# Completing each late unit of a mixture of experts in itself, with whole tiles at the end and stores from two queues

## The chip, the cores and the metric

The kernel runs on one core of a Trainium2 chip. The metric is the device time of one execution in microseconds (us). Five engines run their own instruction streams in order and wait for each other through semaphores: TensorE (PE in the rows, PEld for its weight loads), VectorE (DVE), ScalarE (ACT), GpSimd (POOL) and SyncE (SP). DMAs are issued by SP, ACT and POOL and are carried out by 16 DMA engines that the core has to itself.

## The reference

One layer of a streaming encoder on x of 512 tokens by 1024 (float32). Everything before the experts (modulated norm, convolution group, latent attention, output projection, residual) is the same in both kernels but for the queue that loads x first. The part that matters here is the mixture of experts:

```python
def hier_moe(h, w_group, b_group, w_expert, b_expert, w_gate_e, w_up_e, w_down_e):
    ...                                   # top-1 group of 4, top-2 experts of its 8: gates [512, 32]
    y = jnp.zeros_like(h)
    for e in range(N_EXPERTS):            # 32 experts, D_MODEL 1024, D_EXPERT 256
        a = jax.nn.silu(h @ w_gate_e[e]) * (h @ w_up_e[e])
        y = y + gates[:, e:e + 1] * (a @ w_down_e[e])
    return y
# out = x + g_f * hier_moe(norm(x) * (1 + sc_f) + sh_f)
```

Each expert has 1 MB of gate, 1 MB of up and 1 MB of down weights; all 32 are loaded, some 100 MB. Each token goes to two experts.

## The kernel before, in words

The front of the kernel (to about 290 us) computes the modulation, the projections, attention, convolution and the routing. Then the experts come in 12 **units**, in the order `eeellsllsxss`: e and l units hold two experts with 64 places for tokens each, s units four experts with 32 places, and the x unit two experts with 64 + 32 and 32 places. A unit's tokens are gathered from DRAM into a tile of 128 rows (indirect DMA, POOL), and then go through these steps (the class `Unit`, and `combine`):

- `Unit(...)`, L1443: eight transposes on TensorE turn the 128 x 1024 rows; ACT (L1446) and VectorE (`complete`, L1457 and L1458) scale and shift them.
- `gate_up`, L1469: for each of eight slices of the 1024 inputs one matmul per piece of the unit, gate and up side by side in 512 columns. The first four slices need the expert's weight tile "part 0", the last four "part 1". Then silu on ACT (L1472) and a product on VectorE (L1474).
- `turn`, L1481: two transposes of the product, and a copy on ACT (L1483).
- `down`, L1495, in two halves of 512 output columns: matmuls, then VectorE scales with the gate (L1498), ACT rounds to float32r (L1499) and the remainder is taken (L1500, on POOL, in the last unit on VectorE), so that a high and a low part stand in a tile.
- `combine`, L1512: with a one-hot matrix of the unit's tokens (`one_hot`, VectorE, L1451) TensorE spreads the rows to the 512 tokens, in 8 tiles (2 column halves by 4 token tiles), and VectorE adds each tile to x (L1515). Two PSUM banks `f` are used by turns; the last unit uses four (two of them named `tr`). In the last unit each tile is stored by a DMA as soon as it is added (L1517).

The loop at L1560 writes these steps in the order in which each engine runs them: gate and up of unit n, the transposes of unit n + 1, down of unit n - 1, the turn of unit n, and then four tiles of a `combine`, which adds units in pairs. For the last unit the loop runs the rest of the combine before it, places the combine of the unit before between the halves of gate and up, and then runs down half, combine half, down half, combine half.

Weights come through SP alone (`loads_upto`, `load_keys`, L997), in the order part 0, part 1, down of each unit, into a ring of 4 and slots of 15 tiles of 1 MB (`room`); a load waits until its tile was read, and for the eighth load before it. A gate/up tile takes two DMAs of 512 KB, a down tile one of 1 MB. Those of the last unit are cut in halves and interleaved between experts (`LAST`, `cuts`).

Of the kernel before, what the change touches and what calls it, by code (L numbers as in the profile page):

```python
# [41 lines left out]
def hybrid_block(ctx: ExitStack, tc: tile.TileContext, A, out, dbg=None, stop=None):  # L42
    nc = tc.nc
    pe, act, dve, pool, sp = nc.tensor, nc.scalar, nc.vector, nc.gpsimd, nc.sync
# [88 lines left out]

    def load_x():
        ts = []
        for i in range(2):
            xt = S([128, 2, 1024])
            for s in range(2):
                sp.dma_start(xt[:, s, :], xv[:, 2 * i + s, :])
            ts.append(xt)  # L140
        return ts

    X = load_x()

# [822 lines left out]

    def load(key, n):

        e, part = key  # L970
        o = Wtile()
        o.room = room.pop(0)
        shape = [128, 2, 1024] if part == "d" else [128, 2, 4, 256]
        o.t = (W if o.room == "r" else S)(shape)
        if isinstance(e, int):
            pick = lambda w: w[e]
        else:
            if part == 0:
                reg_of[e] = sp.value_load(od[0:1, e[1]:e[1] + 1], min_val=0, max_val=31)
            pick = lambda w: w[bass.ds(reg_of[e], 1)].rearrange("e p a b -> (e p) a b")  # L980
        if part == "d":
            ds = [(o.t[:, :, cs], pick(wd)[:, :, cs]) for cs in cuts(1024, n)]
        else:
            ds = [(o.t[:, k, js], pick(w)[:, 4 * part + js.start:4 * part + js.stop, :])
                  for js in cuts(4, n) for k, w in ((0, wg), (1, wu))]
        Wt[key] = o
        per = len(ds) // n
        return [ds[i:i + per] for i in range(0, len(ds), per)]

    def cuts(m, n):  # L990
        return [slice(i, i + m // n) for i in range(0, m, m // n)]

    def load_keys(ks):

        for ds in zip(*[load(key, min(len(ks), 2)) for key in ks]):
            for o, i in sum(ds, []):
                sp.dma_start(o, i)  # L997

# [18 lines left out]
    nxt = [0]  # L1017
    LAST = {(units[-1][2][0], "d"): 4}
    LAST.update({(units[-1][2][i], part): 2 for i in (0, 2) for part in (0, 1)})

    def loads_upto(n):
        while room and nxt[0] < min(n, len(keys)):
            m = LAST.get(keys[nxt[0]], 1)
            if len(room) < m:
                break
            load_keys(keys[nxt[0]:nxt[0] + m])
            nxt[0] += m

# [19 lines left out]
    loads_upto(3)  # L1048
    X[:] = load_x()

# [379 lines left out]
    class Unit:  # L1430
# [3 lines left out]
        def __init__(self, kind, tokf, gate, buf, weights, first=False):  # L1434
            self.pieces, self.gate, self.buf, self.weights = PIECES[kind], gate, buf, weights
            n = self.n = sum(self.pieces[-1][:2])
            self.hg = hg

            chunks = buf.rearrange("p (q j) -> p j q", j=8) if first else buf.rearrange("p (j q) -> p j q", j=8)
            for hf in range(2):  # L1440
                pt = tr()
                for j in range(4):
                    pe.transpose(pt[:, j * n:(j + 1) * n], chunks[:n, 4 * hf + j, :], ident[:n, :n])  # L1443
                if hf == 0:
                    for j in range(4):
                        act.activation(self.hg[:, j, :n], pt[:, j * n:(j + 1) * n], AF.Identity, scale=G2[:, j:j + 1], bias=H2[:, j:j + 1])  # L1446
            self.pt, self.tokf = pt, tokf

# [53 lines left out]

    def combine(us, banks=None, store=False):

        for u_ in us:
            u_.one_hot()
        for hf in range(2):
            for tt in range(4):
                o = banks[tt]() if banks else fb()
                for m, u_ in enumerate(us):  # L1510
# [5 lines left out]
                if store:  # L1516
                    sp.dma_start(out[0, tt * 128:(tt + 1) * 128, 512 * hf:512 * hf + 512], xr)  # L1517
                yield
# [38 lines left out]


    comb, done, side, prev = iter(()), [], over_table(), None
    for n_ in range(len(units)):  # L1560
        last = n_ == len(units) - 1
        if last:
            run(comb)
            run(prev.down())
            comb = combine([prev])
        cur.gate_up(lambda: last and run(comb))
        if n_ == 1:
            run(gate)
        nxt_u = start(n_ + 1)
        if nxt_u:  # L1570
            nxt_u.complete()
        if last:
            cur.turn()
            down, comb = cur.down(dve), combine([cur], (fb, fb, tr, tr), True)
            for hf in range(2):
                run(down, 1)
                run(comb, 4)
            break
        if prev:
            run(prev.down())  # L1580
            done.append(prev)
        cur.turn()
        if len(done) == 2:
            comb, done = combine(done), []
        run(comb, 4)
        if n_ > 1:
            run(side, 1)
        r_ = [Wt[e, part].room for part in (0, 1) for e in units[n_][2]]
        if n_ < 3:
            r_.remove("s")  # L1590
        if n_:
            r_ += [Wt[e, "d"].room for e in units[n_ - 1][2]]
        room += r_
        loads_upto(len(keys))
        prev, cur = cur, nxt_u
    pool_order.close()
# [123 lines left out]
```

## Time and profile before

| | |
|---|---|
| median of 3 runs | 539.66 us (539.51, 542.92, 539.66) |
| profiled execution | 538.74 us, of it 537.1 us from first to last instruction (span) |
| TensorE busy | 488.8 us (91%) |
| VectorE, ScalarE, GpSimd busy | 274.5, 177.7, 124.5 us |
| HBM read | 150.97 MB, 290 GB/s over the span |
| chain of waits that ended last | PE 58%, DMA 19%, DVE 10%, SP's queue 4%, ACT 4% |

A busy share is an average over parts with different limits, and matmuls that wait in the pipeline count as busy. So the stretches and the chain of waits tell more than the 91%. Times in the rows are us from the start of the span.

### The profile page before, as it was taken

The numbers are of one execution on the slowest core, as the hardware profiler recorded it, in microseconds if no ns is written. First come the engines' busy times: TensorE is split into PE (matmuls) and PEld (weight loads), VectorE is DVE, ScalarE is ACT, GpSimd is POOL, SyncE is SP. The second block draws the span as 40 slices with busy tenths as digits, with TensorE's granted clock in tenths as the row PEclk, the third lists the DMA queues.
The fourth block names the chain that finished last, engine by engine and source line by source line (L and its number), as shares of the span: only waits on it lengthen the run. The fifth ranks groups of instructions, "written<-read, shape, count | busy, mean of one in ns | idle before, by whom it ended". The sixth has DMA issues, their size and how long they took to land.

```text
span 537.1 us, 8202 instructions
## 1 busy us (share of the span) xinstructions
PE 488.8 (91%) x2891; PEld 276.2 (51%) x2891; DVE 274.5 (51%) x631; ACT 177.7 (33%) x389; POOL 124.5 (23%) x118
## 2 busy tenths in 40 slices
PE   4989999899999898999998999999999799989962
PEld 4768976535644475788874344444444241424321
DVE  2447789948937765642555234334453150415532
ACT  4233744015675556721545222210222020211010
POOL 3220570008644534100001022211222020101100
PEclk9999999999999889999998999999999899999988
DMA  8999539986951252286878989999999999999973
GB/s 257 302 320 308 169 131 316 378 304 191 264 187 40 69 207 91 80 306 231 324 242 307 324 316 392 333 416 405 384 414 392 418 409 414 411 408 317 338 264 123
DMA packets 61763, 154.42 MB, mean 287 GB/s; under 512 B 7657, under 2 KB 27257, under 8 KB 56080
## 3 DMA queue, kind: packets, MB, share of 16 engines
q1 hardware_dynamic: 58288, 147.03, 77.3%
q0 software_dynamic: 1888, 4.00, 2.3%
q10 hardware_dynamic: 1536, 2.77, 1.4%
q8 instruction: 25, 0.41, 0.3%
q14 instruction: 26, 0.21, 0.1%
HBM read 150.97 MB, written 4.77 MB: 290 GB/s over the span
## 4 chain that ended last, share of the span: by engine, by line
PE 58%; DMA 19%; DVE 10%; SPq 4%; ACT 4%; issue 2%; POOL 1%; DVEq 0%; ACTq 0%; POOLq 0%
PE acc L1469 12%; PE acc L1495 7%; PE f L1512 6%; DMA s<-in_w_up_e_dram 6%; DMA s<-in_w_down_e_dram 5%; PE acc L116 5%; PE acc L118 4%; PE acc L117 4%; DMA s<-in_w_ada_dram 2%; DVE dw L346 2%; PE f L334 2%; SPq L167 2%; DMA w<-in_w_up_e_dram 2%; DMA w<-in_w_ada_dram 2%; PE tr L1443 2%
## 5 line engine op out<-in xcount | busy, mean ns | idle before, releaser
L1469 PE MATMUL acc<-s,gw 128*32 128x512 f32 (+1 forms) x392 | 94.1, 604 | 1.5 <-DMA s<-in_w_up_e_dram 1.5
L116 PE MATMUL acc<-s,s 128*128 128x512 f32 (+3 forms) x160 | 63.3, 395 | 1.0 <-DVE s L774 1.0
L1512 PE MATMUL f<-s,t 128*128 128x512 f32 x184 | 49.5, 417 | 10.7 <-DVE t L1451 8.1
L118 PE MATMUL acc<-s,s 128*128 128x512 f32 (+3 forms) x160 | 58.8, 368 | 0.0
L117 PE MATMUL acc<-s,s 128*128 128x512 f32 (+3 forms) x160 | 58.8, 368 | 0.0
L1469 PE MATMUL acc<-w,gw 128*32 128x512 f32 (+1 forms) x136 | 54.4, 636 | 3.1 <-DMA w<-in_w_up_e_dram 3.0
L1474 DVE TENSOR_TENSOR t<-t,acc 128x256 f32<-128x256 f32 x12 | 5.1, 421 | 92.5 <-ACT t L1472 92.5
L346 DVE SCALAR_TENSOR_TENSOR dw<-s,cwh,dw 128x512 f32<-128x512 f32 x60 | 50.0, 849 | 1.2
L1469 PEld LDWEIGHTS acc<-s,gw 128*32 128x32 f32 (+1 forms) x392 | 24.9, 124 | 49.6 <-issue 49.5
L1472 ACT ACTIVATE t<-acc 128x256 f32<-128x256 f32 x12 | 4.6, 384 | 129.2 <-PE acc L1469 129.2
L1500 POOL TENSOR_TENSOR s<-t,s 128x512 fp32r<-128x512 f32 x22 | 28.5, 1294 | 75.9 <-ACT s L1499 75.5
L1515 DVE TENSOR_TENSOR s<-s,f 128x512 f32<-128x512 f32 x52 | 35.3, 688 | 20.7 <-PE f L1512 20.7
L1512 PEld LDWEIGHTS f<-s,t 128*128 128x128 f32 x184 | 31.7, 191 | 27.0 <-DVE s L1515 7.1
L1495 PE MATMUL acc<-s,t 128*32 128x512 f32 (+1 forms) x200 | 44.7, 599 | 0.5 <-ACT t L1483 0.5
L116 PEld LDWEIGHTS acc<-s,s 128*128 128x128 f32 x160 | 30.2, 189 | 14.8 <-issue 7.9
L1427 POOL DMA_INDIRECT s<-xg,sidx x11 | 11.2, 1022 | 107.0 <-PE tr L1443 76.6
L1499 ACT CAST s<-t 128x512 fp32r<-128x512 f32 x24 | 14.8, 618 | 53.3 <-DVE t L1498 53.3
L118 PEld LDWEIGHTS acc<-s,s 128*128 128x128 f32 x160 | 30.1, 188 | 4.1
L117 PEld LDWEIGHTS acc<-s,s 128*128 128x128 f32 x160 | 30.3, 189 | 3.3 <-issue 0.2
L1498 DVE SCALAR_TENSOR_TENSOR t<-acc,rt,gw 128x512 f32<-128x512 f32 x24 | 18.0, 751 | 24.8 <-PE acc L1495 24.8
L871 ACT ACTIVATE t<-acc,sm,qs 128x128 f32<-128x128 f32 (+3 forms) x32 | 19.7, 617 | 21.9 <-DVE sm L869 18.6
L868 DVE TENSOR_REDUCE sm<-acc 128x1 f32<-128x128 f32 (+3 forms) x32 | 15.5, 486 | 20.1 <-PE acc L867 20.0
(311 smaller groups left out, 814.4 us busy)
## 6 DMA issues: line engine op xcount, KB each, us to landing
s<-in_w_down_e_dram SPq DMA_DIRECT2D x21, 1024.0 KB, 11.3
s<-in_w_gate_e_dram SPq DMA_DIRECT2D x41, 512.0 KB
s<-in_w_up_e_dram SPq DMA_DIRECT2D x41, 512.0 KB, 10.2
w<-in_w_ada_dram SPq DMA_DIRECT2D x16, 1024.0 KB, 9.2
w<-in_w_gate_e_dram SPq DMA_DIRECT2D x15, 512.0 KB
w<-in_w_up_e_dram SPq DMA_DIRECT2D x15, 512.0 KB, 9.3
w<-in_w_down_e_dram SPq DMA_DIRECT2D x7, 1024.0 KB, 4.9
s<-in_w_ada_dram SPq DMA_DIRECT2D x6, 1024.0 KB, 11.4
```

The costliest lines, as they stand in the source:

```text
L116: pe.matmul(o, lh, rh, start=start, stop=False)
L117: pe.matmul(o, lh, rl, start=False, stop=False)
L118: pe.matmul(o, ll, rh, start=False, stop=stop)
L346: dve.scalar_tensor_tensor(dw[:, t, :], u[:, t // 2, k:k + 512], w, dw[:, t, :], op0=OP.mult, op1=OP.add)
L868: dve.tensor_reduce(H["mx"][:, qt:qt + 1], p[:, :n], axis=AX.X, op=OP.max)
L871: act.activation(e[:, :n], p[:, :n], AF.Exp, scale=qs[:, qt, h:h + 1], bias=H["nb"][:, qt:qt + 1], accum_out=H["rs"][:, qt:qt + 1])
L1469: pe.matmul(gu[sl, :], self.hg[:, j, sl], w.t[:, :, j % 4, :], start=(j == 0), stop=(j == 7), tile_position=(0, o_), skip_group_check=True)
L1495: pe.matmul(o[o_:o_ + w_, :], self.aT[:, n * c + o_:n * c + o_ + w_], w.t[:, c, hs], start=(c == 0), stop=(c == 1), tile_position=(0, o_), ...
L1498: dve.scalar_tensor_tensor(yf[:n], o[:n], self.gate, gf[:n, hs], op0=OP.mult, op1=OP.mult)
L1500: eng.tensor_tensor(self.yhl[:n, 1, hs], yf[:n], self.yhl[:n, 0, hs].bitcast(F32), op=OP.subtract)
L1512: pe.matmul(o, u_.ot[:u_.n, tt * 128:(tt + 1) * 128], u_.yhl[:u_.n, k, 512 * hf:512 * hf + 512], start=(m == 0 and k == 0), stop=(m == len ...
L1515: dve.tensor_tensor(xr, xr, o, op=OP.add)
```

## The change

Four things change. (1) From the sixth unit on (`SOON = 5`), down follows the turn of the same unit, and the unit is combined alone: four of its tiles between the halves of the next unit's gate and up, four after the next unit's turn. Units 1 to 4 are still combined in pairs, unit 5 alone. (2) The last unit's weights are loaded as all others, in whole tiles; its one-hot matrix is made ahead of down, and both halves of down are run before the combine. (3) The eight stores go out from SP and ACT by turns. (4) The four first loads of x are issued by ACT instead of SP.

```diff
-    def load_x():
+    def load_x(eng):
...
-                sp.dma_start(xt[:, s, :], xv[:, 2 * i + s, :])
+                eng.dma_start(xt[:, s, :], xv[:, 2 * i + s, :])
...
-    X = load_x()
+    X = load_x(act)
...
         if part == "d":
-            ds = [(o.t[:, :, cs], pick(wd)[:, :, cs]) for cs in cuts(1024, n)]
-        else:
-            ds = [(o.t[:, k, js], pick(w)[:, 4 * part + js.start:4 * part + js.stop, :])
-                  for js in cuts(4, n) for k, w in ((0, wg), (1, wu))]
...
+            return [(o.t, pick(wd))]
+        return [(o.t[:, k], pick(w)[:, 4 * part:4 * part + 4, :]) for k, w in ((0, wg), (1, wu))]
...
-    LAST = {(units[-1][2][0], "d"): 4}
-    LAST.update({(units[-1][2][i], part): 2 for i in (0, 2) for part in (0, 1)})
-
     def loads_upto(n):
         while room and nxt[0] < min(n, len(keys)):
...
+            for o, i in load(keys[nxt[0]]):
+                sp.dma_start(o, i)
+            nxt[0] += 1
...
-    X[:] = load_x()
+    X[:] = load_x(sp)
...
-    def combine(us, banks=None, store=False):
+    def combine(us, banks=(fb,) * 4, store=False):
 
         for u_ in us:
-            u_.one_hot()
+            if not u_.ot:
+                u_.one_hot()
...
-                    sp.dma_start(out[0, tt * 128:(tt + 1) * 128, 512 * hf:512 * hf + 512], xr)
+                    (act if tt % 2 else sp).dma_start(out[0, tt * 128:(tt + 1) * 128, 512 * hf:512 * hf + 512], xr)
...
+    SOON = 5
     comb, done, side, prev = iter(()), [], over_table(), None
     for n_ in range(len(units)):
         last = n_ == len(units) - 1
-        if last:
-            run(comb)
-            run(prev.down())
-            comb = combine([prev])
-        cur.gate_up(lambda: last and run(comb))
+        cur.gate_up(lambda: n_ >= SOON and run(comb, 4))
...
-        if last:
-            cur.turn()
-            down, comb = cur.down(dve), combine([cur], (fb, fb, tr, tr), True)
-            for hf in range(2):
-                run(down, 1)
-                run(comb, 4)
-            break
         if prev:
             run(prev.down())
             done.append(prev)
         cur.turn()
-        if len(done) == 2:
-            comb, done = combine(done), []
-        run(comb, 4)
+        if n_ < SOON:
+            if len(done) == 2:
+                comb, done = combine(done), []
+            run(comb, 4)
+        else:
+            run(comb)
+            if done:
+                run(combine(done))
+            if last:
+                comb = combine([cur], (fb, fb, tr, tr), True)
+                cur.one_hot()
+                run(cur.down(dve))
+                run(comb)
+                break
+            run(cur.down())
+            comb, done = combine([cur]), []
...
-        if n_:
+        if prev:
             r_ += [Wt[e, "d"].room for e in units[n_ - 1][2]]
+        if n_ >= SOON:
+            r_ += [Wt[e, "d"].room for e in units[n_][2]]
         room += r_
         loads_upto(len(keys))
-        prev, cur = cur, nxt_u
+        prev, cur = cur if n_ < SOON else None, nxt_u
```

Line numbers of the changed kernel differ: L1469, L1481, L1495, L1512 and L997 of before are L1451, L1463, L1477, L1495 and L1008 there.

TensorE at the end of unit 11's gate and up (`acc_4181` before), before the change: the eight transposes of unit 12's rows (`tr_...<-ident,s`) are followed by unit 10's down.

```order
L1469 MATMUL acc_4181<-w_4142,gw 32x512
L1443 MATMUL tr_4217<-ident,s_2166 128x128 x4
L1443 MATMUL tr_4226<-ident,s_2166 128x128 x4
L1495 MATMUL acc_4234<-s_3981,t_4113 64x512
L1495 MATMUL acc_4234<-s_3981,t_4113 32x512
L1495 MATMUL acc_4234<-s_3983,t_4113 32x512
```

And the same place with the change (the turn is L1463, combine L1495, down L1477).

```order
L1425 MATMUL tr_4344<-ident,s_2166 128x128 x4
L1425 MATMUL tr_4353<-ident,s_2166 128x128 x4
L1463 MATMUL tr_4360<-ident,t_4341 128x128 x2
L1495 MATMUL f_4365<-s_4215,t_4307 128x512 x2
L1495 MATMUL f_4369<-s_4215,t_4307 128x512 x2
L1495 MATMUL f_4373<-s_4215,t_4307 128x512 x2
L1495 MATMUL f_4377<-s_4215,t_4307 128x512 x2
L1477 MATMUL acc_4382<-w_4128,t_4363 32x512
L1477 MATMUL acc_4382<-s_4130,t_4363 32x512
```

Unit 11's own turn comes right after the transposes, then four tiles of unit 10 alone, and then unit 11's own down; another unit's down no longer stands between.

TensorE at the end of the last unit, before the change: four tiles of the first half (`f`, `tr`) are added between the two halves of down (L1495).

```order
L1495 MATMUL acc_4476<-s_4340,t_4473 32x512
L1512 MATMUL f_4491<-s_4475,t_4489 128x512 x2
L1512 MATMUL f_4496<-s_4475,t_4489 128x512 x2
L1512 MATMUL tr_4501<-s_4475,t_4489 128x512 x2
L1512 MATMUL tr_4506<-s_4475,t_4489 128x512 x2
L1495 MATMUL acc_4511<-s_4337,t_4473 32x512
L1495 MATMUL acc_4511<-w_4338,t_4473 32x512
```

With the change (down is L1477, combine L1495).

```order
L1477 MATMUL acc_4506<-w_4426,t_4485 32x512
L1477 MATMUL acc_4519<-s_4420,t_4485 32x512
L1477 MATMUL acc_4519<-s_4422,t_4485 32x512
L1477 MATMUL acc_4519<-s_4424,t_4485 32x512
L1477 MATMUL acc_4519<-w_4426,t_4485 32x512
...
L1495 MATMUL f_4532<-s_4505,t_4503 128x512 x2
L1495 MATMUL f_4537<-s_4505,t_4503 128x512 x2
L1495 MATMUL tr_4542<-s_4505,t_4503 128x512 x2
L1495 MATMUL tr_4547<-s_4505,t_4503 128x512 x2
L1495 MATMUL f_4552<-s_4505,t_4503 128x512 x2
```

The second half of down (`acc_4519`) now follows the first without a tile of the combine between them, and the eight tiles come after both.

## Rows read from the trace of the kernel before

**Rows 1.** The page's second section: load on the DMA engines in 40 slices.

```profile
DMA  8999539986951252286878989999999999999973
GB/s 257 302 320 308 169 131 316 378 304 191 264 187 40 69 207 91 80 306 231 324 242 307 324 316 392 333 416 405 384 414 392 418 409 414 411 408 317 338 264 123
```

**Rows 2.** Table by stretches: length, each engine's busy time, clock, DMA share, GB/s.

```profile
391.00:484.00 93.00, 86.09 (x436) 31.09 (x434) 29.02 (x46) 15.76 (x38) 13.46 (x11) 0.98 1.02 409
484.00:510.00 26.00, 24.26 (x136) 10.79 (x136) 14.25 (x22) 2.46 (x5) 5.12 (x4) 1.00 0.95 327
```

**Rows 3.** The chain of waits: start, duration, what. From 441 to 474 us.

```profile
441.39 12.37 DMA s<-in_w_down_e_dram
...
464.00 10.15 DMA w<-in_w_up_e_dram
```

**Rows 4.** The list of DMA issues: size of each, median us to landing.

```profile
s<-in_w_up_e_dram SPq DMA_DIRECT2D x41, 512.0 KB, 10.2
...
s<-in_w_up_e_dram SPq DMA_DIRECT2D x12, 256.0 KB, 6.1
```

**Rows 5.** The chain of waits from unit 6 on; the 450.68 row from the timeline.

```profile
368.57 7.00 PE acc L1469 x64
375.57 1.02 PE tr L1443 x8
376.60 3.58 PE acc L1495 x16
...
380.55 3.84 PE f L1512 x16
...
450.68 8.01 PE L1469 MATMUL acc<-s,gw 128*64 128x512 f32 x24
...
478.90 7.99 PE acc L1495 x24
...
503.20 0.68 PE f L1512 x2
...
507.73 1.34 PE f L1512 x4
```

**Rows 6.** The last unit: chain of waits, one stretch (clock 0.50), timeline of DVE.

```profile
514.59 1.97 PE acc L1495 x16
...
516.58 0.76 DVE t L1498
...
518.01 0.69 DVE s L1500
...
519.25 2.04 PE f L1512 x4
...
520.00:522.00 2.00, 2.00 (x7) 1.51 (x6) 1.35 (x2) 0.00 (x0) 0.00 (x0) 0.50 0.00 0
...
528.75 1.28 DVE L1515 TENSOR_TENSOR s<-s,tr 128x512 f32<-128x512 f32 x2
```

**Rows 7.** The stores' line: durations, first and last start; time to landing.

```profile
L1517 SPq DMA_DIRECT2D out_dram<-s x8: 332/350/1158, 521.2 to 530.6; - x8
...
DMA to landing us min/median/max: 2.0/2.7/3.3
```

**Rows 8.** The start: stretches, then the timeline of SP, ACT and PE.

```profile
0.00:5.00 5.00, 1.23 (x4) 0.93 (x4) 0.48 (x4) 1.49 (x2) 1.69 (x7) 1.00 0.61 177
5.00:10.00 5.00, 1.61 (x8) 1.61 (x9) 1.13 (x4) 2.52 (x5) 1.63 (x4) 1.00 0.94 303
...
1.36 1.84 SPq L139 DMA_DIRECT2D s<-in_x_dram  x4
3.24 3.33 SPq L157 DMA_DIRECT2D s<-in_w_ada_dram  x2
...
5.55 1.06 ACT L209 ACTIVATE xh<-s 128x1024 f32<-128x1024 f32 x1 [2.12 <-DMA s<-in_x_dram]
...
27.45 1.92 PE L222 MATMUL tr<-s,cs 128*32 128x256 f32 x28 [1.56 <-DMA s<-in_w_ada_dram]
```

More of the change, by code (lines that the diff above doesn't have):

```diff
@@ L966, in hybrid_block, with load @@
         pass
-    def load(key, n):
+    def load(key):
         e, part = key
@@ L980, in load @@
             pick = lambda w: w[bass.ds(reg_of[e], 1)].rearrange("e p a b -> (e p) a b")
+        Wt[key] = o
         if part == "d":
-            ds = [(o.t[:, :, cs], pick(wd)[:, :, cs]) for cs in cuts(1024, n)]
-        else:
-            ds = [(o.t[:, k, js], pick(w)[:, 4 * part + js.start:4 * part + js.stop, :])
-                  for js in cuts(4, n) for k, w in ((0, wg), (1, wu))]
[L986 to L997, printed above, removed]
+            return [(o.t, pick(wd))]
+        return [(o.t[:, k], pick(w)[:, 4 * part:4 * part + 4, :]) for k, w in ((0, wg), (1, wu))]
     PIECES = {2: [(0, 64, 0), (64, 64, 1)], 4: [(32 * i, 32, i) for i in range(4)],
@@ L1017, in hybrid_block @@
     nxt = [0]
-    LAST = {(units[-1][2][0], "d"): 4}
-    LAST.update({(units[-1][2][i], part): 2 for i in (0, 2) for part in (0, 1)})
     def loads_upto(n):
         while room and nxt[0] < min(n, len(keys)):
-            m = LAST.get(keys[nxt[0]], 1)
-            if len(room) < m:
-                break
-            load_keys(keys[nxt[0]:nxt[0] + m])
-            nxt[0] += m
+            for o, i in load(keys[nxt[0]]):
+                sp.dma_start(o, i)
+            nxt[0] += 1
     dve.scalar_tensor_tensor(G2, G2, 1.0, col("nf"), op0=OP.add, op1=OP.mult)
@@ L1446, in __init__ @@
                         act.activation(self.hg[:, j, :n], pt[:, j * n:(j + 1) * n], AF.Identity, scale=G2[:, j:j + 1], bias=H2[:, j:j + 1])
-            self.pt, self.tokf = pt, tokf
+            self.pt, self.tokf, self.ot = pt, tokf, None
         def one_hot(self):
@@ L1501, in down @@
                 yield
-    def combine(us, banks=None, store=False):
+    def combine(us, banks=(fb,) * 4, store=False):
         for u_ in us:
-            u_.one_hot()
+            if not u_.ot:
+                u_.one_hot()
         for hf in range(2):
             for tt in range(4):
-                o = banks[tt]() if banks else fb()
+                o = banks[tt]()
                 for m, u_ in enumerate(us):
@@ L1571, in hybrid_block @@
             nxt_u.complete()
-        if last:
-            cur.turn()
-            down, comb = cur.down(dve), combine([cur], (fb, fb, tr, tr), True)
-            for hf in range(2):
-                run(down, 1)
-                run(comb, 4)
-            break
         if prev:
```

## The prediction

> **What bounds the kernel now.** I read the page first. Its second section gives the load on the DMA engines in 40 slices of 13.4 us [rows 1]: from the 27th slice on they are full, at 384 to 418 GB/s, until the last four slices sink to 317, 338, 264 and 123. The reader is to see both: a long full stretch, and an end that is not full though nothing but loading is left to do. The table by stretches says it in numbers [rows 2]: from 391 to 484 us the share is 1.02 at 409 GB/s; from 484 to 510 us it is 0.95 at only 327 GB/s.
>
> Then the chain of waits. From 441 to 474 us it consists of loads alone [rows 3]: the last down weights of unit 10 of 12 (units counted from 1; e and l units have 2 experts, s units 4) land at 441.39 + 12.37 = 453.76 us, the last gate and up weights of unit 11 at 464.00 + 10.15 = 474.15 us. Between these lie 16 loads of 512 KB, 8.39 MB in 20.39 us, 411 GB/s. So in the middle TensorE waits for weights and the stream sets the pace. After 474 us the chain is TensorE and what follows it, to the end [rows 5, 6].
>
> Why is the stream slow at the end? The list of DMAs [rows 4] shows the up loads of 512 KB landing a median 10.2 us after issue, those of 256 KB after 6.1 us. The second kind is the last unit's, which are cut in halves. SP keeps eight loads in flight (each waits for the eighth before it): 8 x 0.524 MB in 10.2 us is 411 GB/s, 8 x 0.262 MB in 6.1 us is 344 GB/s. With half the bytes in flight and packets of half the size, the same eight loads don't fill the engines.
>
> **The change part by part.**
>
> *Last unit in whole tiles.* The order of the loads is the same, so up to 474 us I take the stream as it is. Unit 11's down weights (4.19 MB) and the whole of unit 12 (12.58 MB) follow at the measured 411 GB/s: 474.15 + 10.2 = 484.35, and 484.35 + 30.6 = **514.9 us** for the very last tile. Before, at 327 GB/s, the last piece comes at up to 484.35 + 38.5 = 522.8. But the last unit's first half of down began at 514.59 us [rows 6], because in halves the first half needs only half of the tiles. So the load side of this start moves by +0.3 us and no more: what the faster stream gains is used up by waiting for whole tiles. The bounds are 514.9 and, if whole tiles go no faster than halves, 522.8; I take the first, since its rate is that of 16 loads of the same size just before.
>
> The Trainium skill, page "Perfetto Trace Analysis", section "DMA Optimizations", advises splitting a DMA so that some of it starts sooner, where the engines are idle; this change does the opposite. By that rule the last down would start at up to 522.8 and the kernel would gain nothing. The share of 0.95 to 1.02 [rows 2] says the engines are not idle, so the rule's condition isn't met here.
>
> *Units 6 to 12 completed in themselves.* TensorE does the same matmuls, but down follows its own gate and up, and each unit is added to x by itself. Does TensorE still arrive by 514.9? From 368.57 us, where unit 6 starts in both orders [rows 5]:
> - gate and up: six units at 7.00 = 42.0, unit 10 (pieces of 64 and 32) two halves of 8.01 = 16.0;
> - transposes 6 x 1.02 = 6.1; turns 7 x 0.45, with 0.2 each for what they wait, 4.5;
> - down: six times 3.6 = 21.6 (unit 5's among them), unit 10's 8.0;
> - adding units: four tiles of the pair 3 and 4 at 4.1 (3.84 without its wait); unit 5 alone, behind its own down, 1.3 of waiting and 5.9; units 6 to 11, 12 halves of 2.9. A unit alone costs more than half a pair: from 503.20 to 509.07 us it took 5.87 for eight tiles, paced by VectorE's adds, where half a pair's eight took about 3.9.
> The sum is 144, and the last turn has nothing to hide behind (about 1 us): 368.6 + 145 = **513.6 us**. A tie with the stream; I take 514.9, and the range has to hold TensorE some us late. VectorE's 24 additional adds (15 us at 0.64) lie in these halves.
>
> Does this order starve the stream? A load also waits until its buffer was read. Down weights now come free a unit earlier, and by the sum above TensorE finishes the first half of unit 11's gate and up near 484 us and the second near 491, while unit 12's loads into those buffers land from about 497 us (gate and up, after 484.35 and 10.2 for the first half) and 509 us (down) on, and are issued some 10 and 12 us before that, at 487 and 497. So nothing is late, with 3 to 6 us to spare.
>
> *The tail.* Before: down half, scale, round, subtract, one-hot, add four tiles, and only then the second half's down [rows 6], from 514.59 to the last add at 530.03. Now both halves of down run together: 3.6 us. VectorE's scale starts at +1.99, the subtract ends at +4.1 (518.70 - 514.59); the second scale, round and subtract, 2.1 us, end at +6.25; then eight adds at 0.645 (1.28 a pair), bound by VectorE, end at +11.4. Before it was 15.4: **-4.0 us**. Bounds: -4.1, and 0 if TensorE falls to 1.2 GHz, as it did from 519 to 522 us after 2.7 us of waiting [rows 6]: then down takes 7.2 and the eight tiles 8 more.
>
> *Stores from two queues.* From the last add to the end were 7.1 us; the last store was issued 0.6 us after it, and the stores took 2.0 to 3.3 us to land [rows 7]. Now SP and ACT issue by turns, so the last leaves at once: **-1.1 us**, between +1.5 (eight stores in 5 us instead of two groups of four) and -2.
>
> *First loads of x on ACT.* SP's first w_ada load moves from 3.24 to about 1.36 us [rows 8]. ACT's first work on x was at 5.55 us and had waited 2.12 us for it, so the four issues (1.84 us on SP) find room there. The engines' share was 0.61 in the first 5 us, of which 1.4 pass before x is issued at all, and 0.94 in the next 5, so they were nearly full once started. What waits behind is TensorE, 1.56 us at 27.45 us, for w_ada. I take **-0.5 us**, between +0.5 (x arrives later, mixed with w_ada) and -1.9 (all of the earlier issue).
>
> The Trainium skill, page "DMA: Bandwidth & Descriptors", section "Issuing engines are not separate DMA queues", says that DMAs from several engines share the same 16 engines and save only issue time. By it this term would be 0 and the forecast 0.5 us later; the traces of before cannot decide it.
>
> *The rest* (SP's shorter loader, the one-hot set early) costs nothing: it lies under SP's and VectorE's waits.
>
> **Sum.** -0.5 + 0.3 - 4.0 - 1.1 = -5.3 us. The profiled execution took 538.74 (span 537.1), so 533.4 on its own scale; it lies 0.92 under the median of 539.66, so for a median **534.3 us**, 1.0% faster. A measurement here tells about 1% from no change, that is 534.3 and 545.1: the forecast stands on the line.
>
> **Rivals.**
> 1. *The start and the stores give their full amounts* (-1.9, -2): 532.0. For: the chain begins with SP's issues. Against: the share of 0.94. Chance 0.15.
> 2. *The tail doesn't pay*: whole tiles go slower than 411 GB/s, or TensorE waits for the last tile and drops to 1.2 GHz. 2 to 8 us are lost: 536 to 542. For: the engine did drop at 519; against: 16 loads at 411. Chance 0.18.
> 3. *TensorE becomes the bound and the kernel is slower.* From unit 6 on there is no other unit's down between gate/up and turn, and 56 tiles are added one by one on two banks. If VectorE paces a tile at 1.0 instead of 0.73 us (it also has 1.5 us of scaling per unit, and the next unit's activations), 15 us come on top of 513.6: last down at 528.6, time 548. It decides from 514.9 on, and costs over 1% once it is 11 us late. For: 0.73 already is above TensorE's 0.5. Against: that work stands in VectorE's 11 us of gate, turn and down. Chance 0.10.
> The forecast keeps 0.57: from 532 (its terms at their gaining ends) to 538 (TensorE 2 us late at the last down, the stores at +1.5 in place of -1.1). The range for 8 in 10 is 531 to 540: rival 1 less the 0.9 us by which the executions shown scatter (538.74 to 539.66), and up to rival 2 at 5.7 of its 8 us. Faster by over 1%: half of the forecast and rival 1, about 0.44; slower: 0.11; within: 0.45.
>
> **What will show it.** The last unit's up loads should land after about 10 us in place of 6.1, and the rate from 484 to 514 us be about 409. TensorE should hardly wait for weights between 391 and 474. The last down should start at 514 to 516 and the last add come 11 to 12 us later. If that start is past 518 because TensorE arrives late, the sum of matmuls was wrong; if a weight load ends the wait, the rate was.

## The result and the profile after

The changed kernel took **534.95 us** (median of 4 runs, 532.28 to 537.63) beside 540.49 us (4 runs, 539.51 to 542.92) of the kernel before: ratio 0.987 (95% interval 0.983 to 0.991). In a second comparison, with 8 and 31 runs, it was 536.23 beside 541.98, ratio 0.990 (0.987 to 0.994). So it is about 1% faster. The profiled execution took 534.46 us, span 532.9; before it was 538.74 and 537.1. The forecast was 534.3.

The lines of the program have moved: gate and up are now L1451, turn L1463, down L1477, scaling L1480 to L1482, the matmuls that add a unit to x L1495, the adds L1498, the stores L1500.

The page's second section [rows 1]:

```profile
GB/s 270 302 320 310 156 122 325 368 330 174 247 228 9 73 237 92 75 271 220 361 197 321 292 355 371 317 405 413 398 415 408 411 413 411 410 417 409 414 162 164
```

The full stretch now reaches to the 38th slice at 398 to 417 GB/s, and then the load stops at once: the sinking slices of before (317, 338, 264) are gone. The stretches say the same [rows 2] (columns: length, busy time of TensorE, its weight loads, VectorE, ScalarE, GpSimd, clock, DMA share, GB/s):

```profile
391.00:484.00 93.00, 87.36 (x433) 30.01 (x434) 39.37 (x63) 15.22 (x34) 15.06 (x13) 1.00 1.02 412
484.00:510.00 26.00, 24.09 (x174) 8.80 (x164) 11.65 (x18) 3.53 (x9) 3.27 (x3) 1.00 1.02 409
516.00:533.00 17.00, 6.59 (x33) 3.00 (x25) 7.58 (x12) 1.24 (x2) 0.00 (x0) 0.80 0.35 129
```

409 GB/s stand where 327 stood. The packets of the DMAs differ too, from 484 to 510 us, first before, then with the change:

```profile
DMA packets 4613, 8.50 MB, mean 327 GB/s; under 512 B 481, under 2 KB 481, under 8 KB 4609
DMA packets 2426, 10.65 MB, mean 409 GB/s; under 512 B 268, under 2 KB 268, under 8 KB 1987
```

Before, the packets that carry weights have 2 KB in this stretch and take 0.094 us in the mean; now most have 4 KB and take 0.163 us. In the list of DMAs all up loads are of 512 KB now [rows 4]:

```profile
s<-in_w_up_e_dram SPq DMA_DIRECT2D x49, 512.0 KB, 10.9
```

The chain of waits around the last unit [rows 6]:

```profile
512.54 1.34 PE f L1495 x4
513.88 2.24 PE acc L1477 x16
...
516.14 0.76 DVE t L1480
...
520.30 3.60 DVE s L1498 x6
...
524.36 0.73 DVE s L1498 x2
```

The last down begins at 513.88 (514.59 before), directly behind TensorE's own matmuls. The loads of [rows 3] have left the chain, which now shares the span so (page, fourth section; DMA was 19%):

```profile
PE 69%; DVE 13%; DMA 6%; ACT 4%; SPq 3%; issue 2%; POOL 1%; DVEq 0%; ACTq 0%; POOLq 0%
```

The last add ends at 525.09, 11.2 us later; before it was 15.4. And TensorE's list of waits, from 376 us to the end (us in total, times, longest):

```profile
PE f L1495 <- DVE s L1498: 5.4, 16, 0.8
PE tr L1463 <- DVE gw L1439: 3.9, 5, 0.8
```

Two more waits of 1 us follow; none for weights is among them (only the weight loads of the last down sat idle 0.2 us for a DMA). New is the second line: five turns wait 0.78 us each for VectorE, which completes the next unit's rows. The stores [rows 7] and the start [rows 8]:

```profile
L1500 SPq DMA_DIRECT2D out_dram<-s x4: 332/338/349, 520.9 to 524.5; - x4
L1500 ACTq DMA_DIRECT2D out_dram<-s x4: 338/342/348, 521.5 to 525.1; - x4
...
DMA to landing us min/median/max: 2.1/3.3/4.5
```

```profile
1.35 1.95 SPq L157 DMA_DIRECT2D s<-in_w_ada_dram  x2
...
0.91 2.43 ACTq L139 DMA_DIRECT2D s<-in_x_dram  x4
6.74 1.06 ACT L209 ACTIVATE xh<-s 128x1024 f32<-128x1024 f32 x1 [0.19 <-DMA s<-in_x_dram]
```

The last store leaves with the last add (525.1). From the last add to the end are 7.8 us, not 6.0 as forecast (7.1 before). The view gives a time to landing for some of the stores only; by the semaphore events in the trace the last store lands 4.6 us after the last add and the end of the span comes 3.2 after that. Before these were 5.1 and 2.0.

What SP does behind its last store is in the rows of its own instructions, before and with the change:

```profile
L1632 SPq COMPARE_BRANCH  x1: 53/53/53, 532.0 to 532.0; - x1
L1632 SPq EVENT_SEMAPHORE  x9: 17/17/17, 534.8 to 535.4; - x9
L1716 SPq EVENT_SEMAPHORE  x14: 17/28/28, 535.5 to 537.1; - x14
```

```profile
L1620 SPq COMPARE_BRANCH  x1: 53/53/53, 526.0 to 526.0; - x1
L1620 SPq EVENT_SEMAPHORE  x9: 17/17/17, 529.1 to 529.7; - x9
L1704 SPq EVENT_SEMAPHORE  x14: 17/28/28, 529.8 to 532.8; - x14
```

It reads a count and jumps (`COMPARE_BRANCH`) over the code for tokens that found no place in a unit, stands still, and then goes through the last waits. In the trace the jump ends 0.98 us after the last add (before 2.04), SP stands for 3.03 us behind it (2.78) and a second time for 1.38 us among the last waits (before not at all), and the remaining waits take 2.4 (2.3): 7.8 us and 7.1. The wait for the last store is passed at 529.71, at the moment of its landing (529.69; before 535.17 and 535.15) and in step with the waits around it.

At the start, the first w_ada load goes out at 1.35 instead of 3.24 us, yet x arrives 1.2 us later than before (6.74, not 5.55) and unit 6 starts at 368.53 (368.57 before).

### The profile page after: what moved, and what is told of

Read it like the earlier page. It is cut to its first block, busy times and chain, and to the rows that moved or that the text cites. A ratio compares the mean times of both kernels' runs of the same rounds, so it can differ in the third digit from the quotient of the medians.

```text
span 532.9 us, 8170 instructions
## 1 busy us (share of the span) xinstructions
PE 486.2 (91%) x2891; PEld 272.9 (51%) x2891; DVE 289.0 (54%) x655; ACT 178.3 (33%) x389; POOL 124.4 (23%) x118
## 4 chain that ended last, share of the span: by engine, by line
PE 69%; DVE 13%; DMA 6%; ACT 4%; SPq 3%; issue 2%; POOL 1%; DVEq 0%; ACTq 0%; POOLq 0%
PE acc L1451 18%; PE acc L1477 9%; PE f L1495 8%; PE acc L116 5%; PE acc L118 4%; PE acc L117 4%; DVE s L1498 3%; DVE dw L346 2%; PE f L334 2%; DMA s<-in_w_ada_dram 2%; PE tr L1425 2%; DMA w<-in_w_ada_dram 2%; PE f L574 2%; PE acc L899 2%; DMA xg<-t 2%
## 5 line engine op out<-in xcount | busy, mean ns | idle before, releaser
L1451 PE MATMUL acc<-s,gw 128*32 128x512 f32 (+1 forms) x408 | 92.5, 597 | 0.0
L1498 DVE TENSOR_TENSOR s<-s,f 128x512 f32<-128x512 f32 x76 | 49.6, 685 | 35.9 <-PE f L1495 35.9
L1495 PE MATMUL f<-s,t 128*128 128x512 f32 x184 | 54.4, 425 | 8.8 <-DVE s L1498 5.4
L1451 PEld LDWEIGHTS acc<-s,gw 128*32 128x32 f32 (+1 forms) x408 | 24.6, 122 | 46.7 <-issue 44.8
L1451 PE MATMUL acc<-w,gw 128*32 128x512 f32 (+1 forms) x120 | 48.2, 622 | 0.0
L1482 POOL TENSOR_TENSOR s<-t,s 128x512 fp32r<-128x512 f32 x22 | 28.2, 1281 | 85.1 <-ACT s L1481 79.1
L1495 PEld LDWEIGHTS f<-s,t 128*128 128x128 f32 x184 | 30.0, 188 | 33.0 <-DVE s L1498 16.9
L1477 PE MATMUL acc<-s,t 128*64 128x512 f32 (+1 forms) x184 | 44.5, 598 | 0.0
L1481 ACT CAST s<-t 128x512 fp32r<-128x512 f32 x24 | 14.8, 618 | 63.7 <-DVE t L1480 56.7
L1480 DVE SCALAR_TENSOR_TENSOR t<-acc,rt,gw 128x512 f32<-128x512 f32 x24 | 18.0, 750 | 25.0 <-PE acc L1477 25.0
## 6 DMA issues: line engine op xcount, KB each, us to landing
s<-in_w_ada_dram SPq DMA_DIRECT2D x6, 1024.0 KB, 11.2
```

The lines of the kernel that those rows point to most:

```text
L1451: pe.matmul(gu[sl, :], self.hg[:, j, sl], w.t[:, :, j % 4, :], start=(j == 0), stop=(j == 7), tile_position=(0, o_), skip_group_check=True)
L1477: pe.matmul(o[o_:o_ + w_, :], self.aT[:, n * c + o_:n * c + o_ + w_], w.t[:, c, hs], start=(c == 0), stop=(c == 1), tile_position=(0, o_), ...
L1480: dve.scalar_tensor_tensor(yf[:n], o[:n], self.gate, gf[:n, hs], op0=OP.mult, op1=OP.mult)
L1482: eng.tensor_tensor(self.yhl[:n, 1, hs], yf[:n], self.yhl[:n, 0, hs].bitcast(F32), op=OP.subtract)
L1495: pe.matmul(o, u_.ot[:u_.n, tt * 128:(tt + 1) * 128], u_.yhl[:u_.n, k, 512 * hf:512 * hf + 512], start=(m == 0 and k == 0), stop=(m == len ...
L1498: dve.tensor_tensor(xr, xr, o, op=OP.add)
```

## The experiments

**Theory A**, mine after the result: the gain is the tail of the last unit, which needs whole tiles; TensorE and the stream of weights tie at the last down; start and stores gave nothing. Its rivals are named in the expectations. The marks are in this table; each is of one execution, and so are differences between them. From the profiled execution: "last add" counts from the start of unit 6 to the end of the last add, "landing" from there until the last store has landed (semaphore events), "rest" from there to the end of the span.

| kernel | median, us | ratio to before (95%) | unit 6 starts | last add | landing | rest |
|---|---|---|---|---|---|---|
| before | 541.98 / 540.84 / 542.50 | 1 | 368.57 | 161.5 | 5.1 | 2.0 |
| the change | 534.95 | 0.987 (0.983 to 0.991) | 368.53 | 156.6 | 4.6 | 3.2 |
| e0, the change again | 536.23 | 0.990 (0.987 to 0.994) | 369.34 | 157.1 | 4.5 | 3.3 |
| e1, x on SP | 537.61 | 0.993 (0.990 to 0.997) | 367.45 | 156.9 | 4.5 | 3.5 |
| e2, stores from SP | 537.01 | 0.992 (0.989 to 0.995) | 369.20 | 157.4 | 4.6 | 4.2 |
| e4, before + whole tiles | 544.49 | 1.006 (1.003 to 1.010) | 370.52 | 162.1 | 5.2 | 5.1 |
| e3, change in halves | 537.51 | 0.991 (0.988 to 0.994) | 368.05 | 159.7 | 4.6 | 2.0 |
| e5, before + whole + tail | 538.95 | 0.996 (0.993 to 0.999) | 370.45 | 157.3 | 4.6 | 4.8 |
| e6, early turn | 537.25 | 0.991 (0.987 to 0.994) | 370.29 | 157.5 | 4.6 | 3.2 |
| e7, early turn, down in halves | 536.73 | 0.992 (0.988 to 0.995) | 368.87 | 156.4 | 4.1 | 5.0 |
| e9, turn in another bank | 537.25 | 0.989 (0.984 to 0.994) | 369.24 | 159.3 | 4.5 | 3.9 |
| e10, the same, down in halves | 535.30 | 0.987 (0.983 to 0.991) | 369.60 | 154.2 | 4.6 | 4.7 |
| e12, half of the stores (2 runs) | 533.39 | 0.984 (0.978 to 0.990) | 368.82 | 157.3 | 4.4 | 2.4 |

e0, e1, e2 and e4 ran beside the first median of before, e3 to e7 (without e4) beside the second, e9 to e12 beside the third.

**e0_change_again.** No edit.

> The changed kernel once more, as the measure for the runs beside it. Theory A (the 5.8 us gained are the last unit's tail, 15.4 to 11.2 us, and 0.7 of an earlier last down; start and stores gave nothing): ratio to the kernel before 0.987 to 0.991, unit 6 begins at 368.3 to 368.8 us, last down at 513.5 to 514.5, last add 11.0 to 11.5 later, 7 to 8 us from there to the end. Theory B (the gain is for the most part luck of the profiled execution, a scatter of 532 to 538 in the runs so far): ratio 0.993 or more.

Ratio and end (7.8 us) are as A says. Unit 6 began at 369.34, 0.5 later than it allows, the last down at 514.66 (145.3 after unit 6), 0.2 later, and the last add came 11.8 after that, 0.3 more. B's 0.993 lies just inside this interval (to 0.994) and outside the first one (to 0.991): that the gain is luck of one execution is unlikely. How far the first 368 us differ from execution to execution was new.

**e1_x_on_sp.** The start undone.

```diff
-    X = load_x(act)
+    X = load_x(sp)
```

> The changed kernel with the first loads of x back on SP, nothing else undone. Theory A (the start gives nothing, because what the weights of ada gain is used up before unit 6): the same as the changed kernel within 0.5 us, unit 6 at 368.3 to 368.9. Theory C (the earlier issue is worth its 0.5 to 1.9 us, and something else has cost the same in the changed kernel): unit 6 at 369.0 to 370.5, and 0.5 to 1.9 us longer.

Neither, as it was put: unit 6 came *earlier*, at 367.45. The chain of waits and the stretches of e1 tell why:

```profile
48.15 1.86 PE tr L222 x32
...
367.45 3.57 PE acc L1451 x32
...
66.00:290.00 224.00, 210.28 (x1302) 137.73 (x1301) 148.55 (x371) 105.43 (x222) 66.28 (x64) 1.00 0.64 218
290.00:366.00 76.00, 72.22 (x405) 33.25 (x405) 29.66 (x78) 21.91 (x56) 17.72 (x16) 1.00 0.95 352
```

and the same of e0:

```profile
47.34 1.86 PE tr L222 x32
...
369.34 3.57 PE acc L1451 x32
...
66.00:290.00 224.00, 211.35 (x1293) 138.74 (x1292) 147.47 (x360) 105.53 (x222) 65.64 (x64) 0.98 0.64 215
290.00:366.00 76.00, 72.69 (x403) 33.31 (x403) 29.17 (x81) 21.91 (x56) 16.93 (x16) 0.98 0.94 345
```

At the transposes of w_ada's last part (L222) e1 is 0.8 us late. Then e1's clock stays at 1.00, in e0 it is 0.98 in both stretches, and e1 needs 319.30 us from there to unit 6 instead of 322.00. The clock of one execution hides the start. So I compared that row in all traces: with x on ACT (nine) 47.34 to 48.00, mean 47.58; with x on SP (before, e1, e4, e5) 47.40, 48.15, 48.30 and 49.56, mean 48.35. The start may be worth **0.8 us** there, with four scattered values on one side; before's profiled execution was the earliest of its kind. At unit 6 nothing of it shows: the means are 369.10 (nine) and 369.25 (four), within a scatter of 3 us. The medians (537.61 against 536.23, intervals of the ratios overlapping) differ C's way. So neither A's "nothing" nor C's amount is shown.

The Trainium skill ("DMA: Bandwidth & Descriptors", "Issuing engines are not separate DMA queues") says that a second issuing engine saves only issue time. Here the earlier issue was 1.9 us of SP's time, of which 0.8 may be seen at 47 us; that the term is then 0, as I had worked out, does not follow from the page.

**e2_stores_sp.** The stores undone.

```diff
-                    (act if tt % 2 else sp).dma_start(out[...], xr)
+                    sp.dma_start(out[...], xr)
```

> The changed kernel with all eight stores of the last unit issued by SP. Theory A (the end is set by how long the last stores take to land, 4.5 us, and not by their issue): last add to end 7.5 to 8.5 us, against 7.8 with two queues, time the same within 0.7 us. Theory D (two queues save the wait in the queue, as forecast, 1.1 us): last add to end 8.9 or more, time 1.1 us longer. If it is under 7.3, two queues cost something.

Last add to end is 8.7 us, between A's bound (8.5) and D's (8.9), 1.0 longer than with two queues; the median is 0.8 longer (intervals overlapping). The last store lands 4.6 us after the last add, as with two queues: the second queue saves nothing that lands. But the end does not wait for the landing, which was A's reason:

```profile
L1620 SPq COMPARE_BRANCH  x1: 53/53/53, 528.3 to 528.3; - x1
L1620 SPq EVENT_SEMAPHORE  x9: 17/17/17, 531.1 to 533.7; - x9
```

SP passes the wait for the last store at 533.67, 2.5 us after it landed (531.20); in e4, e5, e7 and e10 it is 2.8 to 3.4. What counts is when SP is done with the jump: here 1.69 us after the last add and in e5, also from SP alone, 2.01; in the eight kernels with eight stores from two queues 0.96 to 1.11. So at that mark the second queue saves **0.7 to 1.0 us**, near D's amount. Before it was 2.04, with one issue that took 1158 ns [rows 7], and in e4 2.81. Behind the jump SP stands 2.75 us and a second time 2.0; the second is 0 to 2.4 over all kernels and hides D's amount. The trace also shows the tie: here a load ends a wait of 0.2 us within the last down.

```profile
497.14 3.64 PE acc L1477 x32
...
500.80 14.91 DMA w<-in_w_down_e_dram
...
515.75 1.92 PE acc L1477 x13
```

**e4_before_whole.** Only whole tiles: `LAST` and `cuts` taken out of the kernel before, as in the change's diff.

> The kernel before with the last unit loaded in whole tiles and nothing else changed: its order of units, its tail, its stores, its x. Theory A (whole tiles alone give nothing, since the first down half must then wait for whole tiles, to 513.5 to 515 us instead of 514.59): last down at 513.5 to 515.5, tail 15 to 15.5, ratio 0.997 to 1.003. Theory E (the faster stream is the gain): down weights at 514 at the latest and the second half no longer held back, 3 to 5 us shorter, ratio 0.990 to 0.994.

E falls: whole tiles alone gain nothing, the median is rather 0.6% longer. The last down comes 145.6 us after unit 6 (146.0 before), so A was right there; the tail is 16.5 us, 1 longer than A's bound. The chain shows why the faster stream is not used:

```profile
516.12 2.94 PE acc L1477 x16
...
521.75 2.05 PE f L1494 x4
...
525.40 1.92 PE acc L1477 x16
```

The second half of down stands behind the four tiles, in TensorE's queue, 9.3 us after the first, although its weights have landed (517.10): not the loads, but the order holds it back.

**e3_halves.** The change with `LAST` and `cuts` put back.

> The changed kernel with the last unit loaded in halves again, in the order of the kernel before; order of units, tail, stores and x as in the change. Counted from the start of unit 6, the last add came at 161.5 us before and at 156.6 to 157.4 with the change. Theory A (whole tiles are needed: with the same eight loads in flight halves give some 340 GB/s, so the last pieces land about 154 us after the start of unit 6 instead of 145.6, and both halves of down stand behind them): last add at 161 to 164, ratio to the kernel before 0.998 to 1.010. Theory F (the order of the units and of the tail is the whole gain, the size of the loads doesn't matter): last add at 156.5 to 157.5, ratio 0.989 to 0.993.

```profile
484.00:510.00 26.00, 23.61 (x166) 8.73 (x162) 11.77 (x19) 3.89 (x9) 2.79 (x3) 1.00 0.95 331
...
507.89 10.91 DMA w<-in_w_down_e_dram
...
518.85 1.92 PE acc L1495 x10
```

331 GB/s again, as before [rows 2]; the last piece lands 150.8 us after unit 6 and TensorE waits for it. The last add comes at 159.7, 2.3 to 3.1 later than in the five executions with the change's loads and tail. So F's last add falls and A's mechanism holds at this mark, at 3 us where A said 4 to 7. The ratio, though, is F's: the rest was 1.2 us shorter than in the change, without a second standstill of SP, and against its own runs of before the kernel is 3.3 us faster, where e0 is 5.8; the intervals overlap, so the times alone do not tell halves from whole tiles. The Trainium skill ("Perfetto Trace Analysis", "DMA Optimizations") says that a split may help where the engines are generally idle; here their share was 0.95, and the split cost some 3 us at the last add.

**e5_before_whole_tail.** The kernel before with e4's edit and

```diff
-            down, comb = cur.down(dve), combine([cur], (fb, fb, tr, tr), True)
-            for hf in range(2):
-                run(down, 1)
-                run(comb, 4)
+            comb = combine([cur], (fb, fb, tr, tr), True)
+            cur.one_hot()
+            run(cur.down(dve))
+            run(comb)
```

> The kernel before (units completed one unit late, unit 11 before the last unit's gate and up) with only two edits: the last unit in whole tiles, and its tail as in the change (one-hot ahead, both halves of down, then the eight tiles). Theory A (these two parts are the gain; that units are completed in themselves adds nothing): last down 145 to 146 us after the start of unit 6, last add 156.5 to 157.5, ratio 0.989 to 0.993. Theory G (units completed in themselves are needed, to have TensorE at the last down in time or to free the buffers for the stream): last down at 148 or later, last add at 159 or more, ratio 0.995 or more.

```profile
516.04 2.74 PE acc L1477 x19
...
522.98 3.60 DVE s L1498 x6
```

Last down 145.6 us after unit 6, last add 157.3: A by both marks, G falls there. Of the 4.1 to 4.9 us that the change gains from unit 6 to the last add (the change, e0, e1, e2 and e12 have 156.6 to 157.4), 4.2 are these two edits; what completing every unit in itself adds does not stand out from that scatter. The ratio, 0.996, is above A's range and at G's mark: the median is 1.9 us below before's, where e0's is 5.8. A's range left out that this kernel has its stores from SP alone and x on SP, and that SP's second standstill may differ (2.03 us here, 1.38 in the change). In the profiles that is 1.7 to 2.5 of the 3.9 us between the two; the remainder stays open.

**e6_turn_early.** Can both bounds of the last down be moved?

```diff
         nxt_u = start(n_ + 1)
+        if n_ >= SOON:
+            cur.turn()
         if nxt_u:
             nxt_u.complete()
```

> The changed kernel with each unit's transposes of its gated rows (turn) issued ahead of the work that completes the next unit's rows on VectorE, from unit 6 on; this removes TensorE's 0.78 us of waiting at the turn, 5 to 6 times. Theory A (a tie: the stream's last tile lands 145.6 us after the start of unit 6, so TensorE may come up to 4 us earlier and must wait for it): last down at 145 to 145.7, last add at 156.3 to 157, time the same within 0.7 us, and a wait for a weight load ahead of the last down. Theory H (TensorE alone sets the last down): last down at 141 to 142, last add at 152.5 to 153.5, 4 us shorter.

Inconclusive: the edit took no wait away.

```profile
PE tr L1463 <- DVE gw L1439: 4.7, 6, 0.8
```

The pool `tr` has two banks, and the turn still got the one that the completion reads. In unit 6, where the turn now stands ahead of unit 5's down, it costs 1.3 us.

**e7_turn_down_halves.** The same, and the last unit's down tiles as column halves:

```diff
+            m = 4 if keys[nxt[0]] == (units[-1][2][0], "d") else 1
+            ds = sum([load(key) for key in keys[nxt[0]:nxt[0] + m]], [])
+            for hs in (slice(0, 512), slice(512, 1024)) if m > 1 else (slice(None),):
+                for o, i in ds:
+                    sp.dma_start(o[:, :, hs] ..., i[:, :, hs] ...)
```

> The early turn, and the last unit's four down tiles loaded as column halves of 512 KB, the first halves of all four ahead of the second ones; gate and up stay whole. Its second half's subtraction goes to GpSimd. Theory A (loads of 512 KB, eight in flight, keep the 411 GB/s, so halves of down cost the stream nothing and let down begin some 4 us earlier): second halves land at 145.6 us after the start of unit 6, down begins at 141 to 142, last add at 153 to 155, 2 to 4 us less than with the change, ratio to the kernel before 0.983 to 0.988. Theory I (any splitting slows the stream): second halves at 148 or later, last add at 156.5 or more.

A missed, for e6's reason: TensorE came at 146.6, so the early halves could not be used. From there to the last add were only 9.8 us (GpSimd's subtraction leaves VectorE to the adds), which made up e6's loss.

**e9_turn_bank.** The wait taken away by its cause.

```diff
-        def turn(self):
+        def turn(self, bank=tr):
...
-            pt = tr()
+            pt = bank()
...
-        cur.turn()
+        cur.turn(acc if n_ > SOON else tr)
```

> The changed kernel with the turn of units 7 to 12 written to a bank of the pool acc instead of tr, so that it no longer needs the bank that VectorE's completion of the next unit reads (in the kernel with the early turn this bank, not the place in the program, kept the wait). Counted from the start of unit 6, the changed kernel began the last down at 145.3 us, its last weights landed at 145.7 to 146.2, its last add came at 156.6 to 157.2. Theory A (a tie of TensorE and stream): TensorE is 5 x 0.78 = 3.9 us earlier at the last down, the first expert's tile allows a start some us earlier but the last one lands at 145.5 to 146.2 all the same; last add at 156 to 157.2, time the same within 0.7 us, and the end of the wait is a weight load. Theory H (TensorE alone sets the end): last add at 152.7 to 153.3, 4 us shorter.

```profile
PE f L1495 <- DVE s L1498: 7.4, 16, 0.9
PE acc L1477 <- DMA w<-in_w_down_e_dram: 2.4, 1, 2.4
...
500.04 16.17 DMA w<-in_w_down_e_dram
...
516.25 3.30 PE acc L1477 x13
...
516.00:520.00 4.00, 3.75 (x20) 1.01 (x24) 0.43 (x1) 0.00 (x0) 0.00 (x0) 0.58 0.00 0
```

The waits for gw are gone, the adds took back 2.0 of them, and TensorE began the last down 143.6 us after unit 6, 1.7 earlier. H falls: it then stands 2.4 us before the last tile, which lands 147.0 after unit 6 (145.6 to 146.5 in the change, e0, e1, e2 and e12). A's tie is shown, and its price was underestimated: after that wait the granted clock was 0.58 in the mean from 516 to 520 us, so mostly its lower level (1.2 GHz), the 13 matmuls took 3.30 us, where e2's 13 took 1.92, and the last add came at 159.3, 2.1 us *later* than A's limit. So a faster TensorE alone made this tail worse in the profiled execution; the median (537.25, six runs) can't be told from the change's.

**e10_turn_bank_down_halves.** e9's edit with e7's loads and its subtraction on GpSimd.

> The same bank for the turn, and the last unit's four down tiles as column halves of 512 KB, first halves first; the second half's subtraction on GpSimd. Theory A (two bounds, both must move): first halves land at about 141 us after the start of unit 6, the second ones at 145.7 to 146.7; TensorE is at the last down by 141.4; the second half's matmuls end at about 147.7 and the last add comes 6 us later, at 153 to 154.5; 2.5 to 4 us shorter than the change, ratio to the kernel before 0.982 to 0.987. Theory I (halves of down slow the stream, or the end is set elsewhere): last add at 156 or later.

```profile
505.19 10.73 DMA w<-in_w_down_e_dram
...
515.97 1.92 PE acc L1482 x10
...
516.00:520.00 4.00, 4.00 (x19) 1.96 (x19) 2.72 (x5) 1.13 (x2) 0.54 (x1) 1.00 0.00 0
```

As A had it: both bounds moved, second halves at 146.3, clock 1.00, last add at 154.2, the earliest of all. Column halves of 512 KB, in packets of 2 KB, ran at 392 GB/s from 500 to 510 us (e9's whole tiles 415), and the last one did not land late, so I falls. How much of the gain is the subtraction on GpSimd, e10 doesn't tell: in e7, where down did not begin earlier, it came with 9.8 us from the last down to the last add in place of 11.2. 1.5 of the 2.4 to 2.9 us by which the last add is earlier are lost again in the rest (4.7 us), and with a ratio of 0.987 the kernel can't be told from the change (0.987 and 0.990).

**e12_half_stores.** Why was the end no shorter?

```diff
-                if store:
+                if store and hf:
```

> The changed kernel without the stores of the first half of the columns (so half of the output is not written): four stores, alternately from SP and ACT, instead of eight. With eight, from the last add to the end are 7.8 us, the last stores landing 4.5 us after their issue, the first ones after 2.0. Theory J (the stores come closer together than before, one each 0.6 us, and pile up; this is what ate the 1.1 us of the second queue): the last store lands 2.0 to 3.0 us after its issue, last add to end 5.5 to 6.5 us. Theory K (what follows the stores at the end of the program takes the time): last add to end 7.5 to 8 us as before.

```profile
L1500 SPq DMA_DIRECT2D out_dram<-s x2: 343/346/348, 524.4 to 525.6; - x2
L1500 ACTq DMA_DIRECT2D out_dram<-s x2: 347/832/1316, 525.0 to 526.2; - x2
```

J falls: with half as many stores the last one lands 4.4 us after the last add all the same. K is nearer, but its number (7.5 to 8) missed too: last add to end is 6.8 us, since SP is past the jump after 0.76, stands for 2.57 and the second time only for 0.61, this once waiting for a store (landed at 530.56, passed at 530.58).

Why SP's second standstill is 1.4 to 2.4 us in ten kernels, and absent in before and e3, no run has varied. The traces give a lead: during each of the ten a packet of 8 KB runs on a queue of the kind `instruction`, as in the change, where SP stands from 530.05 to 531.44 and the packet runs from 530.24 to 530.62. But such packets run near the end of before and e3 too, so that SP waits for code is a guess.

## Why the prediction was right, and where not

| step | forecast | in the pair of profiles | over all runs |
|---|---|---|---|
| start, up to unit 6 | -0.5 | 0.0 | -0.8 at 47 us, -0.1 at unit 6, in a scatter of 3 |
| start of the last down | +0.3 | -0.7 | -0.7 |
| last down to last add | -4.0 | -4.2 | -3.3 to -4.2 (the change, e0, e1, e2, e12) |
| last add to the end | -1.1 | +0.7 | up to the jump -1.1 (the change, e0, e1); behind it +1.7 to +2.0, open |
| sum | -5.3 | -4.2 | medians -5.5, -5.8 |

That 534.95 lies so near the forecast of 534.3 is in part luck. The pair of profiles differs by 4.2 us, two of the four terms came with the other sign, and the kernel before, put at 539.66, had medians of 540.49 to 542.50. The 1.3 to 1.6 us by which the medians gain more than the pair are not accounted for.

- **Stream.** 409 GB/s against the 411 taken; e3 gives the halves' 331 back. Why halves are slower, the division in the prediction does not say: bytes in flight by time to landing give the rate, whatever the cause. It named two causes, and the smaller packets are the larger one. The rate fell by 20%, the engines' share only from 1.02 to 0.95, by 7%; a packet of 2 KB took 0.094 us and one of 4 KB 0.163, 15% more for each byte. So the engines were nearly full, with packets that carry less. The first half of rival 2 (slower whole tiles) did not come; its second half, the wait and the drop, came in e9.
- **The tie.** TensorE's sum of 145 us from unit 6 was measured as 145.35, the stream's end 145.6 to 146.5 (the change, e0, e1, e2, e12). In the pair TensorE set the start of the last down, 513.88, and not the stream's 514.9 that I took. Two budget lines were off and nearly cancelled: five turns wait 0.78 us, not 0.2, and eight tiles of a unit alone took some 5.3, not 5.8 (493.91 to 496.49 and 503.49 to 506.24 us in the chain). Rival 3 needed VectorE to pace a tile at 1.0 us; TensorE waited for its adds 5.4 us in all, not 15.
- **The tail.** Scale at +2.26 (forecast 1.99), last subtraction done at +6.42 (6.25), eight adds in 4.79 (5.15): 11.2 against 11.4. In e0, e1, e2 and e12, where the last tile landed later, it is 11.5 to 12.1. It is the core of the gain up to the last add, and needs whole tiles and the order together: e4 and e3 have one each and lose 5.5 and 3 there.
- **Units completed in themselves** were forecast as a cost that the stream hides. From unit 6 to the last add neither a cost nor a gain stands out (e5: 157.3, with them 156.6 to 157.4).
- **The stores are the step that failed.** The 1.1 us for the wait in the queue were gained, but only up to the jump: SP is past it 0.98 us after the last add, not 2.04. What follows was in none of my terms, since I had taken the end of the program as fixed: from the jump to the end it grew from 5.1 to 6.8 us, 1.4 of it by SP's second standstill. Its cause stays open. The pile-up that I named for the bound of +1.5 is not borne out by e12.
- **The start** is not settled: -0.5 lies between the 0.8 us at 47 us and the 0.1 at unit 6. Rival 1 (-1.9 and -2) did not come.

## What to carry to other kernels

Splitting loads has a price where the engines are busy: here loads of 256 KB in packets of 2 KB ran at 327 to 331 GB/s, 512 KB in packets of 2 KB at 392, whole tiles at 409 to 415. So look at the packets as well as at the size, and split the last tiles in the order in which they are used. Where the stream and the computing engine tie at the end of a kernel, move them together: in e9 making one faster turned the tie into a wait, and the granted clock fell after it. A gain of 1% is best accounted for from a mark in the middle of the program: the first part alone differed by 3.1 us between executions, more than half of this gain. And follow the issuing engine past the last store: here its jump and its last waits, and not the landing, came last.

## What the runs showed that I had not expected

- Unit 6 started between 367.45 and 370.52 us in kernels whose program up to there differs only in the loads of x. In the earliest the granted clock was 1.00 from 66 to 366 us, in the others 0.98 to 0.99; from the row at L222 to unit 6 it took 319.3 us, the others 320.6 to 322.6.
- The first of the eight stores lands 2.0 us after its issue, the last one after 4.1 to 4.6 in every kernel, also with half as many (4.4, e12). It is a few parts that are late: of the 16 completions of the change's last store 13 come 2.5 to 2.7 us after the issue, the others at 3.0, 3.5 and 4.6.
- From the last landing to the end of the span took 2.0 to 5.1 us, in kernels that do the same there, 0 to 2.4 of it SP's second standstill. As much as half of this change's gain can hide in it.
